# Memory norm inside v's products, mixing and query rounding inside the key/value products, TensorE's order by hand

## The chip, the cores and the metric

The kernel runs on one core of a Trainium2 chip. A core has five engines with instruction streams of their own: TensorE (PE in the profile), VectorE (DVE), ScalarE (ACT), GpSimd (POOL) and SyncE (SP), which issues the DMAs. Each engine works through its stream in order and waits for the others by semaphores. The metric is the device time of one execution in microseconds (us).

## The reference

One layer of a decoder: a half-step feed-forward network, three mixing branches, a half-step feed-forward network. Sequence 1024, width 1024, all in float32. What the change touches is branch A (spatial gating) and branch C (attention into 256 memory tokens):

```python
h = RMSNorm(x); z = h @ W_in            # columns [u | v | c_q | c_kv | k_rope | q_mem | gates]
# A: u * (tril(W_s) v + b), chunks of 128 positions, 8 groups of 64 columns
v = layernorm(gelu(z[v]), ln_g, ln_b).reshape(B, nc, CHUNK, SG_GROUPS, SG_GROUP_DIM)
mixed = jnp.einsum('gts,bcsgd->bctgd', w, v) + b_s.T[None, None, :, :, None]
y_a = u * mixed
# C: cross-attention, 4 heads of 128
q = rmsnorm(q_m.reshape(B, S, MEM_HEADS, MEM_HEAD_DIM), q_norm)
kv = rmsnorm(mem, mem_norm) @ w_kv
k = rmsnorm(kv[..., :MEM_WIDTH].reshape(B, M, MEM_HEADS, MEM_HEAD_DIM), k_norm)
p = softmax(q k^T * MEM_HEAD_DIM ** -0.5);  y_c = p @ kv[..., MEM_WIDTH:]
# merged = sum of sigmoid(gate_i) * (y_i @ W_branch_i);  x = x + merged @ W_out
```

## The kernel before

A float32 product is made of three matmuls (`mm3`, L147 to L149): each operand is split into a rounded high part (fp32r, a cast on ACT, L130) and the rest (a subtraction on DVE, L131), and high·high, low·high and high·low are added up in PSUM. A split of a row thus costs one ACT and one DVE instruction, and a matmul waits for both. `split_gain` (L139, L140) does the same with a factor.

The part around the change runs in this order, and PE goes through it in the middle of the span:

- `sgu` (branch A's gating). `gelu_rows` makes v for half a sequence (512 positions): for each of the 8 slices d of the width, four row blocks, three matmuls each, 96 in all; then Gelu on ACT into the tile `u` (L598). On DVE follow the layer norm's statistics (L634, L635), reciprocal roots in small steps (`rsqrt_steps`, L157 to L168), two passes (L638, L640) and the low half of the split (L131, `v_lo`). This is done for the first half and the second half.
- `mem_norm`, between the two halves in the code: it loads the memory (1 MB, transposed, 256 tokens wide), squares it on ACT (L366, 8 of 128x256) and adds the squares on DVE (L371, 7). After v's products `finish` runs: `token_sums` (a matmul with ones, L380), reciprocal root, `norm_scale` (transposes that spread the factors over the partitions, L392) and `norm_put` (L406 and a split) for 8 slices.
- `mem_kv`: product 1 (keys) and product 2 (values) of the normed memory with 48 matmuls of 512 columns each; `head_norm` on the keys (L670 to L676), `to_feature` (8 transposes, L422; split with a gain).
- Mixing, twice: 8 groups of three matmuls with 256 columns and an ACT copy with bias into a tile `u` (L651); 16 transposes (L657), a product with u (L658) and a split.
- `mem_queries` (L745 squares, L139/L140 rounding, L748 sums of squares on POOL, L751 `pick` matmuls that sum over heads, reciprocal root) and `mem_attention`: scores (S), exponentials on ACT (L778), turning (T, transposes L820) and values (V) for four pairs of row blocks. Between them it takes steps F of a filler, the product of branch A with its weights (`branches`, 16 steps of 12 matmuls).

The pool of `sgu` has one buffer for each name unless said otherwise: the tile `u` exists once, `v_hi` and `v_lo` twice. The order on each engine is set by the framework's scheduler from its own cost figures; `after` adds a dependence that only orders. PE's list of S, T, V and F steps is a request that the scheduler may change. `mm` tiles hold two PSUM banks, `bank` tiles one. All DMAs of this part stand in SP's one queue in the order of issue.

Of the kernel before, what the change touches and what calls it, by code (L numbers as in the profile page):

```python
# [8 lines left out]
F32 = mybir.dt.float32  # L9
# [36 lines left out]
class Kernel:  # L46
# [97 lines left out]
    def mm3(self, out, s, m, first, last, **kw):  # L144

        mmul = self.nc.tensor.matmul
        mmul(out, s[0], m[0], start=first, stop=False, **kw)  # L147
        mmul(out, s[0], m[1], start=False, stop=False, **kw)  # L148
        self.last = mmul(out, s[1], m[0], start=False, stop=last, **kw)  # L149

    def rsqrt_steps(self, v, n):
# [222 lines left out]
    def token_sums(self, acc, late=False, bank=None):  # L374


        n = acc.shape[-1] // P
        b = (bank or self.bank)()[:, :n]
        for t in range(n):
            i = self.nc.tensor.matmul(  # L380
                b[:, t:t + 1], acc[:, t * P:(t + 1) * P], self.ones, start=True, stop=True)
            if late and t == 0:
                self.after(i, self.last)
        return b

    def norm_scale(self, r, late=False, bank=None):


        n = r.shape[-1]
        b = (bank or self.bank)()  # L390
        for t in range(n):
            i = self.nc.tensor.transpose(  # L392
                b[:, t * P:(t + 1) * P], r[:, t:t + 1].to_broadcast([P, P]), self.ident)
            if late and t == 0:
                self.after(i, self.last)
        return b[:, :n * P]

# [196 lines left out]

    def gelu_rows(self, dst, h, w, pairs):


        gelu = lambda d, x: self.nc.scalar.activation(d, x, ACT.Gelu)  # L598
# [8 lines left out]
    def sgu(self, h):  # L607
        nc, a, tc = self.nc, self.a, self.tc
        with tc.tile_pool(name="sgu", bufs=1) as p:
            ln_g = self.bcast_row(p, "ln_g", a["sg_ln_g"], SGW)  # L610
# [10 lines left out]
            vs, norm = [], None  # L621
            for hf in range(2):
                if hf:
                    norm = self.mem_norm()
                vhi, vlo = (p.tile([P, 4, SGW], F32R, name=n, bufs=2) for n in ("v_hi", "v_lo"))
                vs.append((vhi, vlo))
                rows = p.tile([P, 4, SGW], F32, name="u")
                self.gelu_rows(rows, h[hf], w, hf == 0)
                for i in range(0, 4, 2):
# [12 lines left out]
                    self.split(vhi[:, i:i + 2], vlo[:, i:i + 2], v)  # L642
            kv = self.mem_kv(norm())
            yt = [self.split_pair() for _ in range(4)]
            for hf in range(2):
                m, v = p.tile([P, 4, SGW], F32, name="u"), vs[hf]
                for g in range(SGG):
                    b = self.bank()[:, :4 * SGW // SGG].rearrange("p (c d) -> p c d", c=4)
                    cols = slice(g * SGW // SGG, (g + 1) * SGW // SGG)
                    self.mm3(b, (whi[:, g], wlo[:, g]), tuple(x[:, :, cols] for x in v), True, True)  # L650
                    nc.scalar.activation(m[:, :, cols], b, ACT.Identity, bias=self.sg_b[:, g:g + 1])  # L651
                for j in range(4):
                    u = self.row()
                    nc.sync.dma_start(u, self.z[ZU + j][:, hf])
                    b = self.bank()
                    for c in range(4):
                        nc.tensor.transpose(b[:, c * P:(c + 1) * P], m[:, c, j * P:(j + 1) * P], self.ident)  # L657
                    nc.vector.tensor_tensor(u, u, b, op=ALU.mult)  # L658
                    self.split(*(t[:, hf * 512:hf * 512 + 512] for t in yt[j]), u)
        return yt, kv  # L660

# [16 lines left out]
    def mem_norm(self):  # L678


        nc, a = self.nc, self.a
        views = lambda n, dt: [t[:, i].rearrange("p (c m) -> p c m", m=ML)[:, c]
                               for t in (self.h4(dt) for _ in range(n)) for i in range(2) for c in range(2)]
        x4 = [self.h4() for _ in range(2)]
# [7 lines left out]
        hi, lo = views(2, F32R), views(2, F32R)  # L692

        def finish():
            r = self.rms(self.token_sums(acc, late=True), ML // P, D)
            scale = self.norm_scale(r, late=True)
            for c in range(DT):
                self.norm_put(hi[c], lo[c], x[c], self.g_mem[:, c:c + 1], scale)
            return hi, lo

        return finish

    def mem_kv(self, mt):

# [16 lines left out]
        self.head_norm(x, [ps[:, 0], ps[:, 1]])  # L721
        ps = product(w)
        for hh in range(0, MH, 2):
# [6 lines left out]

    def mem_queries(self, p):

# [3 lines left out]
        nc.gpsimd.tensor_scalar(gq, self.mq_g, -MD ** -0.5, None, op0=ALU.mult)  # L736
        qt, b = [], self.bank()[:, :NT * MH]
        for pair in range(MH // 2):
            sq = [p.tile([P, S], F32, name="m4", bufs=3) for n in range(2)]
            for o in range(2):  # L740
                q = self.raw()
                nc.sync.dma_start(q, self.z[ZQ + 2 * pair + o].rearrange("p a w -> p (a w)"))
                qt.append(tuple(p.tile([P, S], F32R, name=n, bufs=MH) for n in ("mq_hi", "mq_lo")))
                for n, t in enumerate(sq):
                    nc.scalar.activation(  # L745
                        t[o * P // 2:(o + 1) * P // 2], q[n * P // 2:(n + 1) * P // 2], ACT.Square)
                self.split_gain(*qt[-1], q, gq)
            nc.gpsimd.tensor_tensor(sq[0], sq[0], sq[1], op=ALU.add)  # L748
            for t in range(NT):
                at = t * MH + 2 * pair  # L750
                nc.tensor.matmul(b[:, at:at + 2], sq[0][:, t * P:(t + 1) * P], self.pick, start=True, stop=True)  # L751
        r = p.tile([P, NT * MH], F32, name="mq_r")
        nc.vector.tensor_copy(r, self.rms(b, NT * MH, MD))
        nr = p.tile([P, NT * MH], F32, name="mq_nr")
        nc.gpsimd.tensor_scalar(nr, r, -1.0, None, op0=ALU.mult)
        return qt, r, nr

    def mem_attention(self, p, queries, kt, vv, filler):

# [4 lines left out]
        def scores(i, k):  # L764
# [42 lines left out]
        yt = [self.split_pair(self.h4) for _ in range(MH)]  # L807
        for f, *x in ((F,), (F,), (F,), (S, 0, 0), (S, 0, 1), (F,), (T, 0, 0), (S, 1, 0), (F,), (T, 0, 1), (S, 1, 1),
                      (F,), (V, 0), (T, 1, 0), (F,), (S, 2, 0), (T, 1, 1), (F,), (S, 2, 1), (F,), (V, 1), (T, 2, 0),
                      (F,), (S, 3, 0), (T, 2, 1), (F,), (S, 3, 1), (F,), (V, 2), (T, 3, 0), (F,), (T, 3, 1), (F,),  # L810
                      (F,), (V, 3)):
            f(*x)
# [149 lines left out]
    def mixer(self, norm):  # L962
# [19 lines left out]

        ya, kv = self.sgu(h)
        with tc.tile_pool(name="mem", bufs=1) as p:
            branch_a = self.branches(0, ya, sink_a)
            queries = self.mem_queries(p)
            yc = self.mem_attention(p, queries, *kv, branch_a)
        each = [(d, f) for d in range(DT) for f in range(2)]
# [974 lines left out]
```

## Time and profile before

| quantity | value |
|---|---|
| time, median of 3 runs | 2222.18 us (2221.76 to 2222.68) |
| time of the profiled execution | 2222.94 us |
| its span (first to last instruction) | 2221.2 us |
| PE busy | 2183.0 us (98%) |
| DVE busy | 1563.5 us (70%) |
| ACT busy | 913.1 us (41%) |
| POOL busy | 249.8 us (11%) |
| mean granted TensorE clock | 0.991 |

A row of a view by line gives the line, engine, operation, tiles, shape and count, then the busy time, the mean of one, and the idle time ahead of it with what ended it. A row of a timeline gives the start, the duration, the instruction and in brackets the wait ahead of it. A row of the windows gives, for a stretch of the span, its length and then for PE, PE's weight loads, DVE, ACT and POOL the busy time (with the count), the granted clock, the share of DMA engines in use and GB/s. Matmuls overlap, so the distance between two starts, not the duration, says what one costs.

### The profile page before, as it was taken

The page shows a single profiled execution, that of the slowest core. Times are in us where ns is not written, and L with a number is a line of the kernel's source. Part 1 is how long each engine was busy: PE and PEld are TensorE (multiplying, and loading weights), DVE is VectorE, ACT ScalarE, POOL GpSimd, SP SyncE. Part 2 cuts the span into 40 slices and gives each one's busy share as a digit, 9 for nine tenths or more (in the row PEclk, how much of TensorE's full clock was granted, in tenths as well). Part 3 has the DMA queues.
Part 4 walks back from the last instruction along what each step waited for, and adds up shares of the span by engine and source line. Part 5 has one row for each costly group of instructions (what it writes and reads, how often), then busy time and mean ns, then how long its engine had stood idle before and what let it go on. Part 6 is the DMA issues. An engine that isn't in the chain of part 4 may idle for free.

```text
span 2221.2 us, 27585 instructions
## 1 busy us (share of the span) xinstructions
PE 2183.0 (98%) x10256; PEld 1819.3 (82%) x10256; DVE 1563.5 (70%) x2406; ACT 913.1 (41%) x1513; POOL 249.8 (11%) x252
## 2 busy tenths in 40 slices
PE   9999999999999999999978999999999999999999
PEld 5788888888887888888857889988888888888887
DVE  7976666579888555545777768885886666657884
ACT  5422222243455333344436448843342222224432
POOL 0012111100000000001300131140002121210000
PEclk9999999999999999999988999999999999999999
DMA  4242333484432333331624650075033333328543
GB/s 144 81 147 96 103 101 106 154 306 149 149 109 95 117 102 114 133 102 44 222 95 152 236 210 30 30 284 202 36 104 110 100 114 100 114 100 299 180 128 104
DMA packets 116086, 294.30 MB, mean 132 GB/s; under 512 B 13680, under 2 KB 22000, under 8 KB 115952
## 3 DMA queue, kind: packets, MB, share of 16 engines
q1 hardware_dynamic: 115952, 292.55, 38.6%
q8 instruction: 80, 1.31, 0.2%
q14 instruction: 54, 0.44, 0.1%
HBM read 206.00 MB, written 86.51 MB: 132 GB/s over the span
## 4 chain that ended last, share of the span: by engine, by line
PE 89%; DVE 7%; ACT 2%; issue 1%; DMA 1%; POOL 0%; SPq 0%; ACTq 0%; DVEq 0%; POOLq 0%
PE one L147 14%; PE one L148 14%; PE one L149 14%; PE bank L147 12%; PE bank L149 12%; PE bank L148 12%; PE mm L149 2%; PE mm L147 2%; PE mm L148 2%; PE bank L902 1%; PE bank L917 1%; PE bank L918 1%; DVE wlo L131 1%; PE bank L422 1%; DVE wlo L136 1%
## 5 line engine op out<-in xcount | busy, mean ns | idle before, releaser
L135 ACT CAST whi<-x 128x1024 fp32r<-128x1024 f32 (+1 forms) x201 | 191.2, 954 | 501.9 <-PE one L148 220.4
L1305 DVE TENSOR_TENSOR t<-t,one 128x512 f32<-128x512 f32 x186 | 127.6, 686 | 244.2 <-PE one L149 243.4
L147 PE MATMUL bank<-h,whi 128*128 128x512 f32 x676 | 263.3, 390 | 0.0
L148 PE MATMUL bank<-h,whi 128*128 128x512 f32 x676 | 263.1, 389 | 0.0
L149 PE MATMUL bank<-h,wlo 128*128 128x512 f32 x676 | 263.0, 389 | 0.0
L136 DVE TENSOR_TENSOR wlo<-x,whi 128x1024 fp32r<-128x1024 f32 (+1 forms) x201 | 239.7, 1194 | 31.7 <-ACT whi L135 31.6
L147 PE MATMUL one<-h,whi 128*128 128x512 f32 x508 | 198.7, 391 | 0.7 <-ACT t L1414 0.7
L149 PE MATMUL one<-h,wlo 128*128 128x512 f32 x508 | 197.7, 389 | 0.0
L148 PE MATMUL one<-h,whi 128*128 128x512 f32 x508 | 197.7, 389 | 0.0
L147 PE MATMUL one<-w,whi 128*128 128x512 f32 x424 | 164.9, 389 | 0.0
L149 PE MATMUL one<-w,wlo 128*128 128x512 f32 x424 | 164.9, 389 | 0.0
L148 PE MATMUL one<-w,whi 128*128 128x512 f32 x424 | 164.9, 389 | 0.0
L130 ACT CAST whi<-w 128x1024 fp32r<-128x1024 f32 (+1 forms) x108 | 95.1, 899 | 144.0 <-PE one L148 62.1
L1707 POOL TENSOR_TENSOR raw<-raw 128x512 f32<-128x512 f32 x38 | 62.9, 1656 | 806.0 <-DVE raw L1553 806.0
L131 DVE TENSOR_TENSOR wlo<-w,whi 128x1024 fp32r<-128x1024 f32 (+1 forms) x108 | 110.1, 1033 | 61.2 <-ACT whi L130 61.1
L149 PEld LDWEIGHTS bank<-h,wlo 128*128 128x128 f32 x676 | 126.9, 188 | 26.4
L148 PEld LDWEIGHTS bank<-h,whi 128*128 128x128 f32 x676 | 126.9, 188 | 26.2
L147 PEld LDWEIGHTS bank<-h,whi 128*128 128x128 f32 x676 | 126.9, 188 | 26.2
L147 PE MATMUL bank<-whi 128*128 128x512 f32 x352 | 136.9, 389 | 0.0
L148 PE MATMUL bank<-wlo,whi 128*128 128x512 f32 x352 | 136.9, 389 | 0.0
L149 PE MATMUL bank<-whi,wlo 128*128 128x512 f32 x352 | 136.9, 389 | 0.0
L147 PEld LDWEIGHTS one<-h,whi 128*128 128x128 f32 x508 | 95.4, 188 | 21.0 <-ACT t L1414 1.1
(372 smaller groups left out, 4898.7 us busy)
## 6 DMA issues: line engine op xcount, KB each, us to landing
x<-in_ffn_w_gu_dram SPq DMA_DIRECT2D x78, 512.0 KB, 5.2
w<-tdt SPq DMA_DIRECT2D x40, 512.0 KB, 4.5
tdb<-raw SPq DMA_DIRECT2D x64, 256.0 KB, 2.1
h<-in_ffn_w_down_dram SPq DMA_DIRECT2D x64, 256.0 KB, 6.0
gate<-raw SPq DMA_DIRECT2D x31, 512.0 KB, 2.6
w<-tdb SPq DMA_DIRECT2D x30, 512.0 KB, 4.7
tdt<-w SPq DMA_DIRECT2D x48, 256.0 KB, 2.1
x<-in_w_gate_dram SPq DMA_DIRECT2D x21, 512.0 KB, 5.7
```

The lines of the kernel that those rows point to most:

```text
L130: self.nc.scalar.copy(hi, src)
L131: return (eng or self.nc.vector).tensor_tensor(lo, src, hi.bitcast(F32), op=ALU.subtract)
L135: self.nc.scalar.copy(hi, src)
L136: return lambda: self.nc.vector.tensor_tensor(lo, src, hi.bitcast(F32), op=ALU.subtract)
L147: mmul(out, s[0], m[0], start=first, stop=False, **kw)
L148: mmul(out, s[0], m[1], start=False, stop=False, **kw)
L149: self.last = mmul(out, s[1], m[0], start=False, stop=last, **kw)
L422: nc.tensor.transpose(b[:m, k * P:(k + 1) * P], s, self.ident)
L902: nc.tensor.transpose(b[:, at:at + P], prs[t][:, kk * P:(kk + 1) * P], self.ident)
L917: nc.tensor.matmul(o, w, pt[0], start=n == 0, stop=False)
L1305: return self.nc.vector.tensor_tensor(out, x, y, op=ALU.add)
L1707: sub = lambda d, x, y: (eng or nc.gpsimd).tensor_tensor(d, x, y, op=ALU.subtract)
```

## The change

Four things are changed. First, `mem_norm` becomes a generator in three steps: the memory is loaded ahead of v's second pair of weights into two larger tiles, squared in 2 ACT instructions of 128x1024 and added up in 3 DVE instructions (128x1024, 128x512, 128x256). The norm's matmuls are put inside v's products by `amid`: the token sums ahead of slice d = 7 of the first half, the spreading of the factors ahead of d = 3 of the second half, and the normed memory is written right after. Second, from the key product to the end of memory attention PE's order is the order of the code (`manual_schedule`); the other engines are still scheduled. Third, mixing is a generator `mix(hf)`, taken between the key product and the value product (matmuls of the first half), inside the value product (its transposes), after it (matmuls of the second half) and after the first step of branch A (its transposes). Fourth, the queries are split into tiles that are used before for other things (`h4`, and `v_hi`/`v_lo` of the halves that are mixed), their squares use the tiles of weights, the softmax rows use four views of `v_hi`/`v_lo`, and the list of S, T, V and F steps is another. The separate pool of memory attention is gone. The tile `u` still exists once.

The core of the diff:

```diff
@@ gelu_rows
-    def gelu_rows(self, dst, h, w, pairs):
+    def gelu_rows(self, dst, h, w, pairs, amid={}):
         for d in range(DT):
+            then = amid[d]() if d in amid else None
             for i in range(4):
                 b = ps[i // 2][:, i % 2] if pairs else ps[i]
-                self.mm3(b, tuple(x[:, i * P:(i + 1) * P] for x in h[d]), w[d], d == 0, d == DT - 1)
+                first = self.mm3(b, tuple(x[:, i * P:(i + 1) * P] for x in h[d]), w[d], d == 0, d == DT - 1)
+                if then:
+                    self.after(first, then)
+                then = None
@@ sgu
+            mem = self.mem_norm()
+            next(mem)
             w = self.load(a["w_v"])
...
+            take(0, {7: lambda: next(mem)})
+            take(1, {3: lambda: next(mem)})
+            m0, m1 = mix(0), mix(1)
+            with tc.manual_schedule(engines={mybir.EngineType.PE}):
+                kv = self.mem_kv(next(mem), (lambda: next(m0, None), lambda: next(m0, None)))
+                rooms = [v8(n).rearrange("p (a b) w -> p a (b w)", a=2) for n in ("v_hi", "v_lo")]
+                queries = self.mem_queries([(x[:, 0], x[:, 1]) for x in rooms])
+                next(queries)
+                next(m1)
...
+                branch = self.branches(0, yt, sink)
+                next(branch)
+                next(m1, None)
+                yc = self.mem_attention(next(queries), rooms, *kv, branch)
@@ mem_norm
+        for n, t in enumerate(x4):
+            sq = self.x4() if n == 0 else sq2
+            nc.scalar.activation(sq, t, ACT.Square)
...
+        nc.vector.tensor_tensor(first, first, sq2, op=ALU.add)
+        nc.vector.tensor_tensor(acc, first[:, 0].rearrange("p (a m) -> p a m", a=2),
+                                first[:, 1].rearrange("p (a m) -> p a m", a=2), op=ALU.add)
+        nc.vector.tensor_tensor(acc[:, 0], acc[:, 0], acc[:, 1], op=ALU.add)
+        yield
...
-        acc = None
-        for c in range(DT):
-            acc = self.norm_feed(acc, x[c], ML)
@@ mem_kv
-        def product(w):
+        def product(w, then=None):
...
+                if d == DT // 2 - 1 and then:
+                    then()
...
         self.head_norm(x, [ps[:, 0], ps[:, 1]])
-        ps = product(w)
+        amid[0]()
+        ps = product(w, amid[1])
@@ mem_attention
-            pr = p.tile([P, MH * ML], F32, name="m4", bufs=3).rearrange("p (h m) -> p h m", h=MH)
+            pr = rooms[t % len(rooms)]
...
-        for f, *x in ((F,), (F,), (F,), (S, 0, 0), (S, 0, 1), (F,), (T, 0, 0), (S, 1, 0), (F,), (T, 0, 1), (S, 1, 1),
...
+                (F,), (F,), (S, 0, 0), (F,), (S, 0, 1), (F,), (T, 0, 0), (S, 1, 0), (F,), (T, 0, 1), (S, 1, 1), (F,),
```

The order on PE around the memory norm, before: behind the last of v's matmuls (into `bank_8647`) stand the token sums and the spread factors, then the key product (`mm_8880`).

```order
L149 MATMUL bank_8647<-whi_8449,h4_5175 128x512
L380 MATMUL bank_8800<-ones_91,t_8614 128x1 [waits Activation_49]
L380 MATMUL bank_8800<-ones_91,t_8614 128x1
L392 MATMUL bank_8817<-ident_86,rs_y_8805 128x128 [waits DVE_49,Activation_49]
L392 MATMUL bank_8817<-ident_86,rs_y_8805 128x128
L147 MATMUL mm_8880<-whi_8850,h4_8637 128x512 [waits PE_49,Activation_49]
```

The same two pairs after the change: the factors (`rs_y_8561`) are spread inside the second half of v's matmuls, ahead of slice 3; the sums (L381) stand likewise inside the first half.

```order
L148 MATMUL bank_8645<-wlo_8446,h4_5158 128x512
L149 MATMUL bank_8645<-whi_8445,h4_5159 128x512
L394 MATMUL mm_8682<-ident_86,rs_y_8561 128x128 [waits DVE_49,Activation_49]
L394 MATMUL mm_8682<-ident_86,rs_y_8561 128x128
L147 MATMUL bank_8642<-whi_8445,h4_5158 128x512
L148 MATMUL bank_8642<-wlo_8446,h4_5158 128x512
```

So no matmul of the norm stands between v's products and the key product any more. The order on PE at the end of the mixing matmuls after the change: behind the key product follow the 8 groups of the first half (`bank_8982` to `bank_9017`), of which the fifth is `bank_9002`; before, the value product stood here, and the mixing followed `to_feature`.

```order
L147 MATMUL bank_8997<-v_hi_8467,x4_8419 128x256 [waits Activation_49]
L148 MATMUL bank_8997<-v_lo_8468,x4_8419 128x256
L149 MATMUL bank_8997<-v_hi_8467,x4_8420 128x256
L147 MATMUL bank_9002<-v_hi_8467,x4_8419 128x256 [waits Activation_49]
L148 MATMUL bank_9002<-v_lo_8468,x4_8419 128x256
L149 MATMUL bank_9002<-v_hi_8467,x4_8420 128x256
```

The mixing's matmuls alternate over four banks, so the fifth group waits for the ACT copy of the first. That copy (now L661) writes the tile `u`, in ACT's order after the change:

```order
L130 CAST v_hi_8639<-u_8641 128x1024 [waits DVE_49]
L784 ACTIVATE wlo_9151<-raw_9152 64x1024 [waits DMAHW1_49,Pool_49]
L130 CAST v_hi_8639<-u_8641 128x1024 [waits DVE_49]
L661 ACTIVATE u_8981<-bank_8982,c_sg_b_3207 128x4x64 [waits DVE_49,PE_49]
L661 ACTIVATE u_8981<-bank_8987,c_sg_b_3207 128x4x64 [waits PE_49]
```

`u_8981` takes the one buffer of `u_8641`, the rows of the second half of v. The first copy's wait on DVE is for the last reading of `u_8641`, the second `v_lo_8640`. In DVE's order after the change the rows ahead of it are these (`rs_y_8785`, `rs_y_8811` the layer norm's factors, `rs_y_8960` and `h4_8948` the key's head norm):

```order
L649 SCALAR_TENSOR_TENSOR u_8641<-u_8641,rs_y_8811,ln_b_8414 128x512 [waits DVE_49]
L649 SCALAR_TENSOR_TENSOR u_8641<-u_8641,rs_y_8811,ln_b_8414 128x512
L167 SCALAR_TENSOR_TENSOR rs_b_8962<-rs_w_8961 128x8 [waits DVE_49]
L131 TENSOR_TENSOR v_lo_8640<-u_8641,v_hi_8639 128x1024 [waits Activation_49]
L169 SCALAR_TENSOR_TENSOR rs_y_8960<-rs_b_8962,rs_y_8960 128x8 [waits DVE_49]
L703 TENSOR_TENSOR h4_8948<-h4_8948,rs_y_8960 128x1024 [waits DVE_49]
L131 TENSOR_TENSOR v_lo_8640<-u_8641,v_hi_8639 128x1024 [waits Activation_49]
```

Between the first statistics of v's first half and that `v_lo` DVE now has the splits of seven of the eight slice pairs of the key and value weights (14 instructions of 128x512), the low halves of the normed memory and the keys' head norm; before, it had four of the pairs (8 instructions) and neither of the others.

More of the change, by code (lines that the diff above doesn't have):

```diff
@@ L146, in mm3 @@
         mmul = self.nc.tensor.matmul
-        mmul(out, s[0], m[0], start=first, stop=False, **kw)
+        i = mmul(out, s[0], m[0], start=first, stop=False, **kw)
         mmul(out, s[0], m[1], start=False, stop=False, **kw)
         self.last = mmul(out, s[1], m[0], start=False, stop=last, **kw)
+        return i
     def rsqrt_steps(self, v, n):
@@ L383, in token_sums @@
                 self.after(i, self.last)
+        self.final = i
         return b
@@ L619, in sgu, with take @@
             self.split(whi, wlo, ws)
+            mem = self.mem_norm()
+            next(mem)
             w = self.load(a["w_v"])
[L621 to L625, printed above, removed]
+            vs, yt = [], []
+            def take(hf, amid={}):
+                vhi, vlo = (v8(n) for n in ("v_hi", "v_lo"))
                 vs.append((vhi, vlo))
                 rows = p.tile([P, 4, SGW], F32, name="u")
-                self.gelu_rows(rows, h[hf], w, hf == 0)
+                self.gelu_rows(rows, h[hf], w, hf == 0, amid)
                 for i in range(0, 4, 2):
@@ L642, in sgu, with mix @@
                     self.split(vhi[:, i:i + 2], vlo[:, i:i + 2], v)
-            kv = self.mem_kv(norm())
-            yt = [self.split_pair() for _ in range(4)]
-            for hf in range(2):
+            def mix(hf):
+                if not yt:
+                    yt.extend(self.split_pair() for _ in range(4))
                 m, v = p.tile([P, 4, SGW], F32, name="u"), vs[hf]
@@ L659, in sgu @@
                     self.split(*(t[:, hf * 512:hf * 512 + 512] for t in yt[j]), u)
-        return yt, kv
+            take(0, {7: lambda: next(mem)})
[7 more added lines that the diff above has]
+                next(m1)
+                rooms = [v8(n, F32) for n in ("v_hi", "v_lo")]
+                rooms = [x.rearrange("p (a h) (b m) -> p a (h b) m", a=2, b=2)[:, k] for x in rooms for k in range(2)]
+                branch = self.branches(0, yt, sink)
+                next(branch)
+                next(m1, None)
+                yc = self.mem_attention(next(queries), rooms, *kv, branch)
+        return yc
     def head_norm(self, x, ps):
@@ L736, in mem_queries @@
         nc.gpsimd.tensor_scalar(gq, self.mq_g, -MD ** -0.5, None, op0=ALU.mult)
-        qt, b = [], self.bank()[:, :NT * MH]
+        qt, ss = [], []
         for pair in range(MH // 2):
-            sq = [p.tile([P, S], F32, name="m4", bufs=3) for n in range(2)]
+            sq = [self.wide(n).bitcast(F32) for n in ("whi", "wlo")]
             for o in range(2):
@@ L742, in mem_queries @@
                 nc.sync.dma_start(q, self.z[ZQ + 2 * pair + o].rearrange("p a w -> p (a w)"))
-                qt.append(tuple(p.tile([P, S], F32R, name=n, bufs=MH) for n in ("mq_hi", "mq_lo")))
+                qt.append(rooms.pop(0) if pair else self.split_pair(self.h4))
                 for n, t in enumerate(sq):
@@ L748, in mem_queries, with mem_attention @@
             nc.gpsimd.tensor_tensor(sq[0], sq[0], sq[1], op=ALU.add)
+            ss.append(sq[0])
+        yield
+        b = self.bank()[:, :NT * MH]
+        for pair, sq in enumerate(ss):
             for t in range(NT):
                 at = t * MH + 2 * pair
-                nc.tensor.matmul(b[:, at:at + 2], sq[0][:, t * P:(t + 1) * P], self.pick, start=True, stop=True)
-        r = p.tile([P, NT * MH], F32, name="mq_r")
+                nc.tensor.matmul(b[:, at:at + 2], sq[:, t * P:(t + 1) * P], self.pick, start=True, stop=True)
+        r = self.const.tile([P, NT * MH], F32, name="mq_r")
         nc.vector.tensor_copy(r, self.rms(b, NT * MH, MD))
-        nr = p.tile([P, NT * MH], F32, name="mq_nr")
+        nr = self.const.tile([P, NT * MH], F32, name="mq_nr")
         nc.gpsimd.tensor_scalar(nr, r, -1.0, None, op0=ALU.mult)
-        return qt, r, nr
-    def mem_attention(self, p, queries, kt, vv, filler):
+        yield qt, r, nr
+    def mem_attention(self, queries, rooms, kt, vv, filler):
         nc = self.nc
@@ L981, in sink_c @@
                 nc.sync.dma_start(mc[d], rows)
[L983 to L987, printed above, removed]
+        with tc.tile_pool(name="sgu", bufs=1) as p:
+            yc = self.sgu(h, p, sink_a)
         each = [(d, f) for d in range(DT) for f in range(2)]
```

39 lines of the change are left out of this document (24 added, 15 removed).

## The prediction

> **What bounds the kernel now.** I read the page's busy shares first (TensorE is busy for 98% of the span), so a change can only win where TensorE waits or runs at a lowered clock. The windows of the stretch from v's products to memory attention show where that is:
>
> ```profile
> 1119.50:1134.00 14.50, 1.61 (x8) 1.15 (x7) 14.50 (x55) 5.70 (x10) 0.00 (x0) 0.59 0.23 73
> 1134.00:1142.50 8.50, 6.22 (x14) 4.49 (x15) 6.59 (x15) 2.31 (x7) 0.00 (x0) 0.50 0.00 0
> ...
> 1161.30:1173.60 12.30, 11.53 (x89) 10.39 (x87) 8.94 (x14) 10.88 (x24) 0.00 (x0) 1.00 0.20 60
> 1173.60:1190.40 16.80, 10.47 (x42) 9.26 (x42) 11.28 (x11) 15.03 (x18) 4.51 (x2) 0.59 0.59 189
> 1190.40:1215.00 24.60, 23.82 (x133) 20.21 (x133) 18.71 (x37) 11.81 (x32) 0.53 (x2) 1.00 0.46 142
> 1215.00:1256.00 41.00, 41.00 (x258) 36.74 (x259) 30.48 (x53) 23.71 (x68) 2.15 (x2) 1.00 0.42 135
> 1256.00:1308.00 52.00, 52.00 (x242) 43.50 (x241) 26.30 (x50) 10.40 (x28) 21.58 (x20) 1.00 0.91 349
> ```
>
> Length less TensorE's busy time is its idle time: 12.9, 2.3, 0.8, 6.3 and 0.8, together 23.1 us. Busy time times (1 − granted clock) is what the clock cost: 1.61 × 0.41 + 6.22 × 0.50 + 10.47 × 0.41 = 8.1 us. So 31.2 us are lost here, the ceiling of any gain. After 1215 TensorE never idles, but from 1256 the DMA engines are 0.91 busy, which leaves little room there for a later start. The chain of waits on TensorE names the losses:
>
> ```profile
> PE bank L392 <- DVE rs_y L168: 8.5, 1, 8.5
> PE mm L147 <- ACT mq_hi L139: 5.2, 2, 4.0
> PE bank L380 <- ACT u L598: 2.4, 1, 2.4
> PE mm L149 <- DVE h L131: 2.3, 1, 2.3
> ```
>
> The first, third and fourth belong to the memory norm behind v's products, the second to the rounding of the queries. But what ends the first is VectorE, and VectorE was not idle:
>
> ```profile
> 1105.40:1138.00 32.60, 17.74 (x73) 13.61 (x71) 32.53 (x103) 14.38 (x26) 0.00 (x0) 0.76 0.25 81
> ...
> 1105.47 1.29 DVE L634 BATCH_NORM_STATS2 bn<-u 128x6 f32<-128x512 f32 x2 [2.96 <-ACT u L598]
> ...
> 1137.83 2.76 DVE L131 TENSOR_TENSOR h<-h,h 128x256 fp32r<-128x256 f32 x8
> ```
>
> It is busy 32.53 of 32.60 us, from the statistics of v's first half to the end of `v_lo` of the second, at 1137.8. That chain, 32.4 us long, is what I follow. TensorE waits only because it needs something that lies on it.
>
> **The memory norm moved into v's products.** It takes away the waits of L380, L392 and L149: 13.2 us. ScalarE's squares and VectorE's adds (8 and 7 before; 2 and 3 now) get cheaper, and off TensorE's path either way. It also moves the memory's two loads ahead of the second pair of v's weights in SyncE's queue. The transfers that this can hold back:
>
> ```profile
> h<-in_mem_dram SPq DMA_DIRECT2D x2, 512.0 KB, 7.7
> raw<-gate SPq DMA_DIRECT2D x4, 512.0 KB, 3.5
> raw<-in_w_branch_dram SPq DMA_DIRECT2D x6, 256.0 KB, 2.9
> ```
>
> Against a 512 KB load at 3.5 us the memory's take 7.7 (transposing). The order now puts the three adds and the norm's small steps ahead of a weight split that v's first half needs and of its statistics. The adds cost about 2.3 us (1.2 for 1024 columns, 0.7 for 512, 0.4 for 256, from the rows below). So VectorE's chain starts later by between 0 and 5 us (all hidden; adds and a late load); I take 2.5, at 1108.0, the adds alone.
>
> **Mixing moved between the products.** A group's copy on ScalarE writes the single tile `u`, so the first copy waits for the last `v_lo` of v's second half, and the fifth group of matmuls waits for the first copy. That is the new wait. That `u` holds its next writer back is seen already: this Gelu, with four banks done, waited for `v_lo`.
>
> ```profile
> 1121.29 2.06 ACT L598 ACTIVATE u<-bank 128x512 f32<-128x512 f32 x4 [0.60 <-DVE v_lo L131]
> ```
>
> When does that `v_lo` end now? The chain gains, by the order on VectorE, 6 splits of weights (14 against 8), the 8 low halves of the normed memory, two sums of the head norm, its scaling, and some ten steps on columns:
>
> ```profile
> L131 DVE TENSOR_TENSOR wlo<-raw,whi 128x512 fp32r<-128x512 f32 x8 | 5.2, 679 | 0.0
> ...
> L131 DVE TENSOR_TENSOR h<-h,h 128x256 fp32r<-128x256 f32 x8 | 2.8, 410 | 0.0
> ...
> L672 DVE TENSOR_REDUCE hn_ss<-t 128x4 f32<-128x512 f32 x2 | 1.4, 686 | 1.7 <-ACT t L670 1.7
> L676 DVE TENSOR_TENSOR h<-h,rs_y 128x1024 f32<-128x1024 f32 x1 | 1.2, 1224 | 0.1
> L164 DVE SCALAR_TENSOR_TENSOR rs_w<-rs_b,rms_v 128x8 f32<-128x8 f32 x2 | 0.3, 166 | 0.1
> ```
>
> 6 × 0.65 = 3.9, then 2.8, 1.4, 1.2, and 10 × 0.08 (half of 166 ns, since they overlap) = 0.8, together 10.1. The ten steps of the memory norm's own root, 0.8, leave the chain, since they now run ahead of it; its eight scalings (L406) are in it both times. That is 9.3 more: the chain is 41.7 us long and ends at 1149.7. There is no gap in it that could take any of this, by the 32.53 of 32.60.
>
> POOL's sum of the queries' squares (2.37 us) now falls into this chain, and VectorE does not run beside it:
>
> ```profile
> 1188.25 2.37 POOL L748 TENSOR_TENSOR m<-m,m 128x1024 f32<-128x1024 f32 x1 [6.22 <-ACT m L745]
> ...
> 1188.85 2.32 DVE L131 TENSOR_TENSOR wlo<-raw,whi 128x512 fp32r<-128x512 f32 x1 [1.51 <-ACT whi L130]
> ```
>
> A split of 0.68 us took 2.32 beside it: 1.64 more. The collision costs between 0 and 2.4 us; I take 1.0, since some of VectorE's instructions there read PSUM or columns. The Trainium skill (SBUF — State Buffer, "SBUF: two separate sides") says that a VectorE instruction with two SBUF inputs and one of GpSimd lock each other out for the whole instruction; these two rows agree, and by that rule the cost would be the full 2.4, so that the time would be 1.4 us longer than the sum below.
>
> ```profile
> 1118.89 0.39 PE L148 MATMUL bank<-wlo,h 128*128 128x512 f32 x1
> 1119.12 0.39 PE L149 MATMUL bank<-whi,h 128*128 128x512 f32 x1
> ...
> 1138.30 0.80 PE L149 MATMUL mm<-whi,h 128*128 128x512 f32 x1 [2.28 <-DVE h L131]
> ...
> 1142.67 0.39 PE L147 MATMUL mm<-whi,h 128*128 128x512 f32 x1
> ...
> 1177.50 0.58 PE L147 MATMUL mm<-h,mq_hi 128*128 128x256 f32 x1 [3.95 <-ACT mq_hi L139]
> ...
> 1203.87 0.28 PE L149 MATMUL mm<-h,mq_lo 128*128 128x256 f32 x1
> 1203.99 0.28 PE L147 MATMUL mm<-h,mq_hi 128*128 128x256 f32 x1
> ...
> 1205.07 1.03 PE L820 MATMUL bank<-ident,m 128*128 128x128 f32 x8
> ```
>
> A matmul of 512 columns takes 0.23 us from start to start (1118.89 to 1119.12), one of 256 columns 0.12. With the first copy (0.5, and as much until its end is seen) TensorE resumes at 1151.7. Without any wait it would reach the fifth group at 1119.35, the end of v's products, + 1.0 (an allowance) for the norm's few small matmuls + 48 × 0.227 for the key product + 12 × 0.12 for four groups = 1132.7. So 19.0 us are lost up to there, wherever the waits lie.
>
> After such an idle time the clock is half: from 1138.30 TensorE ran without a gap and was at the full clock, with 0.39 instead of 0.63 for a matmul, 4.4 us later. Nearly half of that, 2.0 us, is lost at the new restart (between 1.6 and 5.5, the latter if gaps follow, as from 1177.50 to 1190.4, where 10.47 × 0.41 plus the gaps' share was lost). The Trainium skill (TensorE: Matmul & The Clock Gate, "What's actually happening") gives about 3.4 us of idle time for the fall and as much dense work for the return; the wait of 3.95 ahead of 1177.50 and the 4.4 us agree roughly, and by its figure 1.7 us would be lost here.
>
> **Query rounding moved.** The waits on `mq_hi` (5.2), `mq_lo` and the second slow spell go: the queries are rounded while TensorE is in the value product. What is late next is the second mixing. Its first copy stands on ScalarE behind the keys' two gains, a split of a branch weight and the values' cast:
>
> ```profile
> L139 ACT ACTIVATE h<-bank,c_mem_k_norm 128x512 fp32r<-128x512 f32 x2 | 1.3, 684 | 7.0 <-PE bank L422 7.0
> ...
> L130 ACT CAST whi<-raw 128x512 fp32r<-128x512 f32 x28 | 16.4, 625 | 23.1 <-PE mm L149 10.7 <-PE bank L149 6.2 <-DMA raw<-in_mem_w_kv_dram 3.0
> ...
> L130 ACT CAST h<-mm 128x1024 fp32r<-128x1024 f32 x1 | 1.0, 1016 | 0.0
> ...
> L139 ACT ACTIVATE mq_hi<-raw,m_gq 128x1024 fp32r<-128x1024 f32 x4 | 4.6, 1143 | 0.0
> ```
>
> 1.3 + 0.6 + 1.0 + 0.5 = 3.4 us behind the keys' transposes, of which four groups (1.4) cover a part: 2.0 us waited. Two roundings of queries of 1.1 each stand between later copies: 2.0 more. So 4.0 (2 to 6) are lost, in pieces too short for the clock. At the first turn I add 0.7 (VectorE's share of a softmax row is late by one instruction). The new list of steps adds nothing on TensorE, but TensorE can no longer take other work when a softmax row is late, and the DMA engines are nearly full right behind: between 0 and 2 us are given back; I take 0, since the nearest rows, from 1215 to 1308, show TensorE idle for nothing. The tile moves themselves cost nothing: same instructions, same shapes.
>
> **The sum.** Lost before 31.2; after 19.0 + 2.0 + 4.0 + 0.7 = 25.7. The gain is 5.5 us. The profiled execution took 2222.94 us, 0.8 above the median of the runs, 2222.18, and 1.7 above its span: against the median, 2216.7 us. A measurement of this kernel tells about 0.2% (4.4 us) from no change, so this is only just on the faster side.
>
> **The rivals.** (B) A second slow spell, slower than before. The second mixing's first copy also stands behind the split of a branch weight, whose load waits in SyncE's queue behind the last queries' load and several mixing rows. If that load lands late enough that the 2.0 us piece becomes 4 or more, past the 3.95 that were followed by half clock, the clock falls again: the wait itself 2 to 5 (a load of 7.7 instead of 2.9), the clock 5.5 at the rate of the stretch before 1190.4. Together 7.5 to 10.5 more: 2224.2 to 2227.2. For it speaks that this load comes after two 512 KB loads in series; against it that the stretch had the DMA engines only 0.2 to 0.6 busy.
>
> (C) Faster: the wait on `u` comes out shorter. If the chain starts where it did (−2.5), POOL's sum hits nothing (−1.0), and the copies of the second mixing run ahead of the transposes (−2 to −4), the gain is 11 to 13: 2209 to 2211. The chain's arithmetic speaks against more, since VectorE has no gap to shorten.
>
> (D) The list of memory attention gives something back, by softmax rows that come late:
>
> ```profile
> L773 DVE TENSOR_REDUCE m_mx<-mm 128x4 f32<-128x1024 f32 x4 | 4.8, 1207 | 0.0
> L783 DVE TENSOR_TENSOR m<-m,m_rs 128x1024 f32<-128x1024 f32 x3 | 3.7, 1222 | 0.2
> ```
>
> A turn follows its scores by a reduction (1.2), four exponentials and a scaling (1.2), some 4 to 5 us in all; a filler step of 12 matmuls (12 × 0.227 = 2.7) covers most of it. Three such waits of 2 us make 2222.7, no change; with five it is 2226.7, slower. Against it: the first two turns have one step F more ahead of them than before. That the change does not do what it says is not open: the orders show the matmuls in their new places.
>
> **How the numbers follow.** The forecast has 0.55 (0.36 faster by over 0.2%, 0.19 within, since its own range, 2212 to 2221, straddles the bound), B 0.20 (0.13 slower, 0.07 within), C 0.13 (all faster), D 0.12 (0.05 within, 0.07 slower). That makes 0.49 faster, 0.31 within 0.2%, 0.20 slower. The range 2209 to 2227 takes in most of B, C and D; what it leaves out is C's best and B's worst, and mishaps together.
>
> **What would show it.** Right: no wait of L394 longer than 1 us; one wait of about 15 us on the fifth mixing group, ended by ScalarE's copy (L661), which itself waits for `v_lo`; VectorE busy nearly throughout from 1108 to 1150; half clock for some 4 us after; the first turn at about 1201 (1205.1, less 31.2 − 25.7 = 5.5, plus 1.3 for twelve matmuls that are 0.11 dearer than those they replace ahead of it). Wrong: that wait under 10 us or over 20, a granted clock below 0.7 again after 1165, turns that wait in memory attention, or TensorE idle behind 1215.

## The result: no change that can be measured

The changed kernel takes 2222.57 us (median of 12 runs, 2221.14 to 2223.38), the kernel before 2222.34 us in the same runs: the ratio is 1.000, with a 95% interval from 0.9991 to 1.0009. A gain of 5.5 us to 2216.7 was forecast. The span of the profiled execution is 2221.0 us (2221.2 before), the mean granted clock 0.992 (0.991).

The waits of TensorE from 1070 to 1320 in the changed kernel: who waits, for whom, us in all, times, the longest.

```profile
PE bank L147 <- ACT u L661: 14.3, 2, 13.4
PE mm L147 <- ACT v_lo L821: 3.2, 1, 3.2
PE mm L148 <- DVE wlo L131: 2.5, 1, 2.5
PE bank L147 <- DVE h L140: 2.2, 1, 2.2
PE mm L147 <- ACT v_hi L821: 1.2, 1, 1.2
PE mm L147 <- DVE a_mx L923: 1.0, 1, 1.0
PE bank L863 <- DVE m_mx L817: 0.8, 1, 0.8
PE mm L147 <- ACT v L524: 0.2, 1, 0.2
```

All waits of the memory norm behind v's products (8.5, 2.4, 2.3, 2.0) and those on the query rounding are gone. In their place stands one of 13.4 us, on the copies into `u`, and some of 1 to 3 us, two of them in memory attention, where before there was only one, of 0.2 us. (The wait on `a_mx` was there before too, 1.0 us.) Four rows of TensorE's timeline give the places, and a row of the windows for VectorE:

```profile
1149.97 0.58 PE L147 MATMUL bank<-v_hi,x 128*128 128x256 f32 x1 [13.36 <-ACT u L661]
...
1169.43 0.39 PE L147 MATMUL bank<-v_hi,x 128*128 128x256 f32 x1 [2.16 <-DVE h L140]
...
1200.35 1.06 PE L863 MATMUL bank<-ident,v_hi 128*128 128x128 f32 x8 [0.82 <-DVE m_mx L817]
...
1237.27 0.39 PE L147 MATMUL mm<-h,h 128*128 128x256 f32 x1 [3.20 <-ACT v_lo L821]
```

```profile
1106.00:1149.40 43.40, 30.61 (x142) 25.39 (x140) 43.14 (x119) 24.62 (x40) 2.56 (x1) 0.88 0.41 133
```

The first turn is at 1200.35; it was at 1205.07. So 4.7 us were in hand there, and 6.0 if the 1.3 us of dearer work ahead of it is counted. The first scores of the causal attention follow later, ahead of them TensorE waits for `a_mx` in both kernels; here the two are level again, 1312.58 before and 1312.38 now:

```profile
1312.58 0.44 PE L147 MATMUL mm<-h,h 96*128 96x384 f32 x1 [0.97 <-DVE a_mx L880]
```

```profile
1312.38 0.44 PE L147 MATMUL mm<-h,h 96*128 96x384 f32 x1 [0.97 <-DVE a_mx L923]
```

So between the two places 4.5 us of the lead and the 1.3 us of work done ahead were given back, 5.8 us in all, in memory attention. The windows of the changed kernel show it: in the first of these rows TensorE is idle for 4.4 us, and the clock falls for a time; before, it was busy for all of 1215 to 1256.

```profile
1205.00:1256.00 51.00, 46.56 (x297) 41.61 (x296) 37.98 (x67) 27.73 (x80) 2.29 (x2) 0.97 0.34 114
1256.00:1308.00 52.00, 52.00 (x233) 43.07 (x232) 23.62 (x44) 9.76 (x26) 20.21 (x19) 1.00 0.89 335
```

### The profile page after: what moved, and what is told of

The parts are those of the page before. It is cut to its first block, busy times and chain, and to the rows that moved or that the text cites. A ratio compares the mean times of both kernels' runs of the same rounds, so it can differ in the third digit from the quotient of the medians.

```text
span 2221.0 us, 27576 instructions
## 1 busy us (share of the span) xinstructions
PE 2180.9 (98%) x10256; PEld 1818.3 (82%) x10256; DVE 1564.4 (70%) x2402; ACT 912.7 (41%) x1507; POOL 249.0 (11%) x252
```

## The experiments

Each is an edit of the changed kernel, and all compute the whole reference. The kernel before took 2222.3 to 2222.6 us beside them.

**Rows of their own.** The rows of v's second half stand in two tiles of another pool instead of `u`.

```diff
-                rows = p.tile([P, 4, SGW], F32, name="u")
+                rows = [self.x4() for _ in range(2)] if hf else p.tile([P, 4, SGW], F32, name="u")
...
-                    v = rows[:, i:i + 2]
+                    v = rows[i // 2] if hf else rows[:, i:i + 2]
```

> The changed kernel, with the rows of v's second half in two tiles of the x4 kind instead of the tile u, so that mixing's copies need not wait for them. Theory 1 (the single tile u makes the 13.4 us wait, and what lies behind it is free by 1152): the wait on the fifth mixing group falls under 2 us; the value product runs in its place; TensorE then waits 1 to 3 us for the keys' head norm or v_lo, since VectorE's chain ends at about 1150 as before; the first turn comes 8 to 12 us earlier (1188 to 1192 instead of 1200.3), and the time falls by 4 to 12 us to about 2214. Theory 2 (the wait moves on: the queries' loads and roundings on ScalarE and VectorE hold the second mixing and the scores): the first turn comes less than 3 us earlier, the time is within 2 us of 2222.5.

Measured: ratio 0.9963 (0.9951 to 0.9976), median 2212.89 us. The wait on the fifth group is 1.1 us and the first turn at 1194.10. Theory 1 holds for the wait, though the first turn came only 6.3 us earlier, less than the 8 to 12 expected. Two things can account for it, and their shares are open. The traced execution was the slowest of the five, 2217.46 us, and it came to this part 1.3 us later (the first Gelu into `u` starts at 1106.22 instead of 1104.94). And ScalarE's queue has squares of the queries (L784, 1.06 each) between mixing's copies, so that TensorE still has short waits on `u`. Its waits up to 1165:

```profile
PE bank L147 <- ACT u L661: 3.9, 3, 1.8
PE mm L148 <- DVE wlo L131: 2.5, 1, 2.5
PE bank L147 <- DVE h L140: 0.5, 1, 0.5
```

**Another list in memory attention.** From the first value step on a filler step stands again between a turn and the scores behind it.

```diff
-                (V, 0), (T, 1, 0), (S, 2, 0), (F,), (T, 1, 1), (S, 2, 1), (F,), (V, 1), (T, 2, 0), (S, 3, 0), (F,),
-                (T, 2, 1), (S, 3, 1), (F,), (V, 2), (T, 3, 0), (F,), (T, 3, 1), (F,), (V, 3)):
+                (V, 0), (T, 1, 0), (F,), (S, 2, 0), (T, 1, 1), (F,), (S, 2, 1), (F,), (V, 1), (T, 2, 0), (F,),
+                (S, 3, 0), (T, 2, 1), (F,), (S, 3, 1), (F,), (V, 2), (T, 3, 0), (F,), (T, 3, 1), (F,), (F,), (V, 3)):
```

> The changed kernel with another list of steps from the first value step on: one filler step again between each T and the S behind it. Theory D (the list gives back what was gained: S waits for the exponentials that free its PSUM tile): the waits of 3.2 and 1.2 us on the exponentials go, the half clock around 1237 too, and the time falls by 4 to 6 us, to 2217 to 2218.5. Rival (the stretch from 1256 on, with its DMA engines 0.89 busy, sets the end): TensorE then waits 3 us or more behind 1245, and the time stays within 1.5 us of 2222.5.

Measured: ratio 0.9976 (0.9967 to 0.9985), median 2216.72 us. Both waits on the exponentials are gone, and TensorE is busy throughout at the full clock:

```profile
1205.00:1256.00 51.00, 51.00 (x318) 45.50 (x316) 41.31 (x72) 30.22 (x84) 2.56 (x2) 1.00 0.42 142
```

The first turn (1200.60) and the 13.2 us on `u` are as they were. So the list alone gave back 5.9 us, and the nearly full DMA engines behind 1256 took none of it. How it comes about is seen on ScalarE in the changed kernel, rows of its timeline:

```profile
1233.67 0.59 ACT L130 CAST whi<-bank 128x512 fp32r<-128x512 f32 x1 [3.00 <-PE bank L863]
1234.15 0.38 ACT L130 CAST h<-mm 128x256 fp32r<-128x256 f32 x1
1234.41 0.60 ACT L130 CAST whi<-bank 128x512 fp32r<-128x512 f32 x1
1234.89 0.59 ACT L821 ACTIVATE v_lo<-mm,m_mx,mq_nr 128x256 f32<-128x256 f32 x1
```

ScalarE stands for 3.00 us at the cast of a turn that TensorE has not made yet. Behind the cast stand the four exponentials, and only they free the PSUM tile that the next scores (1237.27) need: there are two such `mm` tiles. With a filler step between, the exponentials are over in time. The shorter wait, 1.2 us at 1220.83, has the same form: ahead of its exponentials ScalarE stood 2.14 us at a cast (`h<-mm`, 1218.20) that waited for VectorE.

**Mixing behind the value product.**

```diff
-                kv = self.mem_kv(next(mem), (lambda: next(m0, None), lambda: next(m0, None)))
+                kv = self.mem_kv(next(mem), (lambda: None, lambda: None))
+                next(m0)
+                next(m0, None)
```

> The changed kernel with the mixing of the first half put behind the value product and the keys' transposes, as before the change; all else as changed. Theory 1 (the chain on VectorE to the last v_lo ends near 1149 whatever TensorE does, and the value product of 11 us fits ahead of it): the wait on the fifth group falls to under 2 us, a wait of 2 to 4 us on the head norm appears ahead of the keys' transposes, the first turn comes 6 to 10 us earlier and the time falls by 4 to 10 us. Theory 2 (mixing earlier is worth its place): the time rises or stays within 2 us of 2222.5, since the query rounding becomes the last.

Measured: ratio 0.9954 (0.9942 to 0.9967), median 2212.58 us, the first turn at 1189.31. Undoing this part of the change gains 10 us, and the first turn comes 11.0 us earlier, a little more than the 6 to 10 expected. The value product fills the time in which TensorE waited for `u`; in the first mixing the wait on `u` is 0.4 us, and ahead of the keys' transposes TensorE waits 0.4 us on the head norm, less than the 2 to 4 expected.

**The memory norm behind v's products.** The norm's two groups of matmuls are taken after v's products; mixing stays.

```diff
-            take(0, {7: lambda: next(mem)})
-            take(1, {3: lambda: next(mem)})
+            take(0)
+            take(1)
+            next(mem)
+            next(mem)
```

> The changed kernel with the memory norm's two groups of matmuls behind v's products, as before the change; mixing stays between the products. Theory 1 (TensorE waits for one chain on VectorE, so a wait ahead of the key product only takes its time from the wait on u): waits of about 8 to 13 us come back ahead of the key product, the wait on the fifth mixing group shrinks by about as much, and the time stays within 3 us of 2222.5. Rival (the norm's move is worth its 13 us by itself): the wait on the fifth group stays over 10 us and the time rises by 8 to 13 us.

Measured: ratio 1.0033 (1.0020 to 1.0045), median 2229.70 us, 7.1 above the changed kernel. This lies between both theories. Its waits up to 1165:

```profile
PE mm L394 <- DVE rs_y L169: 8.4, 1, 8.4
PE bank L147 <- ACT u L661: 5.3, 1, 5.3
PE mm L149 <- DVE h L131: 3.1, 1, 3.1
PE bank L381 <- ACT u L601: 2.7, 1, 2.7
PE mm L147 <- ACT h L130: 2.0, 1, 2.0
```

16.2 us of waits are back, but the wait on `u` falls only by 8.1 us, from 13.4 to 5.3, and the 2.5 us in v's first half go. `v_lo` was done at 1137.6, yet the first copy came at 1156.62, right behind the head norm's four ScalarE instructions (from 1152.39 on, after the late key product) and two squares of queries. So the wait on `u` is not set by VectorE's chain alone; once that is short, ScalarE's order sets it.

**Both out.** The last two edits together.

> The changed kernel with the memory norm's matmuls behind v's products and the first mixing behind the value product, both as before the change; the queries' tiles, TensorE's fixed order and the list as changed. The fourth corner of a square: changed 2222.6, mixing out 2212.6, norm out 2229.7. Theory 1 as amended (the norm's waits of 13 to 16 us cost in full where no wait on u stands behind them to be shortened): 10 to 14 us above mixing out, 2222 to 2227. Rival (the norm's move is worth the same 7 us wherever the mixing stands): 2219 to 2221.

Measured: ratio 1.0018 (1.0009 to 1.0027), median 2225.43 us, 12.9 above mixing out. With that the square is closed: moving the norm into v's products is worth 12.9 us where mixing stands behind the value product and 7.1 where it stands ahead of it; moving the mixing ahead costs 10.0 us with the norm inside and 4.3 with the norm outside. The forecast named both the norm's waits that go and the new wait on `u`, but did not ask what either part would be worth without the other. The account closes: with both parts out the rest of the change costs about 3 us against the kernel before, the norm inside takes 12.9 off, the mixing ahead puts 10.0 on, and that leaves nothing. The list's share of the rest is 5.9 us, by the second experiment, so all else (the queries' rounding, the fixed order) saves about 3 us; this last figure is a difference and was not run by itself.

**The scheduler's order on TensorE.** `manual_schedule` is taken away.

```diff
-            with tc.manual_schedule(engines={mybir.EngineType.PE}):
+            if True:
```

> The changed kernel without the fixed order on TensorE: the scheduler orders it. If the scheduler moves the value product ahead of the mixing groups that wait for u, the wait of 13.4 us shrinks under 5 and the time falls by 5 to 10 us: then the order by hand costs time. If it keeps the mixing there (its own cost figures show no wait), the wait stays near 13 us and the time is within 3 us of 2222.5.

Measured: ratio 0.9951 (0.9939 to 0.9964), median 2211.64 us. The scheduler puts the whole value product between the fourth and the fifth group:

```order
L147 MATMUL bank_8995<-v_hi_8467,x4_8419 128x256 [waits Activation_49]
L148 MATMUL bank_8995<-v_lo_8468,x4_8419 128x256
L149 MATMUL bank_8995<-v_hi_8467,x4_8420 128x256
L147 MATMUL mm_9020<-whi_8916,h4_8685 128x512 [waits PE_49]
L148 MATMUL mm_9020<-wlo_8917,h4_8685 128x512
```

That is the place of the wait on `u`, and it shrinks to 1.7 us at most. The waits on the exponentials (L821) are gone too, so the gain holds both losses. The fixed order, as it is written, costs 11 us, a little more than the 5 to 10 expected.

**Both losses mended, in two ways.** Rows of their own with the list of filler steps, and mixing behind the value product with that list.

> The changed kernel with both edits: the rows of v's second half in tiles of their own (that edit alone: 2212.9) and the list with a filler step between each T and the S behind it (alone: 2216.7). If the two losses are separate, in order on TensorE and neither hidden by the other, the gains of 9.5 and 5.6 add up: 2205.5 to 2209. If the second loss is there only to absorb what the first frees (a bound behind both, such as the transfers from 1256 on), the time stays at 2211 or above.

> The changed kernel with the first half's mixing behind the value product (alone: 2212.6) and the list with filler steps (alone: 2216.7). By the same reasoning 2205 to 2209; it ends within 2 us of the kernel with rows of their own and the same list, since both remove the same wait.

Measured: 0.9932 (0.9920 to 0.9944), 2207.24 us, and 0.9933 (0.9919 to 0.9946), 2207.25 us. The gains add up: 0.9963 × 0.9976 = 0.9939 and 0.9954 × 0.9976 = 0.9930. The two losses are separate, and nothing behind them takes either gain back. Both kernels beat the kernel before and the changed one by 15 us.

**Weights first.** In the last of these, v's weights are issued ahead of the memory's loads.

```diff
-            mem = self.mem_norm()
-            next(mem)
             w = self.load(a["w_v"])
+            mem = self.mem_norm()
+            next(mem)
```

> The kernel of mixing out and the list with filler steps (2207.2), with v's weights issued ahead of the memory's loads: one of the two memory loads then stands behind the third slice pair of v's weights in SyncE's queue. It asks what the wait of 2.6 us in v's first half is, which the change brought. If it comes from the memory's load and its add ahead of the weights' split on VectorE, it falls under 1.5 us and the time to 2204.5 to 2206.5. If it comes from VectorE's q and k work, which stands ahead of both, it stays over 2 us and the time within 1.5 us of 2207.2.

Measured: 0.9924 (0.9910 to 0.9938), 2206.34 us. The time does not tell it from 2207.25; the waits up to 1150 do. First without, then with the edit:

```profile
PE mm L148 <- DVE wlo L131: 2.6, 1, 2.6
PE bank L425 <- DVE h L705: 1.2, 1, 1.2
```

```profile
PE bank L425 <- DVE h L705: 3.2, 1, 3.2
PE mm L148 <- DVE wlo L131: 0.9, 1, 0.9
```

The wait in v's first half loses 1.7 us, and the wait on the head norm, 60 us later, gains 2.0. The memory's load and its add, which stood ahead of that split, were the cause of the first. The time was not won because VectorE's chain did not start any earlier. It starts behind the first Gelu into `u`, and this came 28.5 us after v's first matmul without the edit (1075.07 to 1103.60) and 28.6 with it (1077.60 to 1106.16): it waits for a store, as shown below. What TensorE does not wait for early, it then waits for late.

**Rows of their own and the scheduler's order.**

> The changed kernel with rows of their own for v's second half and no fixed order on TensorE. With the fixed order and the list of the change it took 2212.9, with the fixed order and filler steps 2207.2; with the free order and the single u 2211.6. If the free order is good because it avoids the wait on u and spaces the scores, both of which these edits do by hand, then 2206 to 2211, no better than 2207.2 by more than 1.5. If the order by hand costs something else too, under 2205.

Measured: 0.9935 (0.9921 to 0.9949), 2208.84 us: as good as the mended orders by hand and no better. So no cost of the order by hand beyond the two losses shows.

## Why the prediction was right and wrong

- **What bounds the kernel, and the new wait: right.** The wait of 13.4 us is at the fifth mixing group, for the first copy into `u`, which waits for `v_lo`. "About 15" was forecast. VectorE's chain ran from 1106.00 to 1149.3, busy 43.14 of 43.40 us; the forecast had 1108.0 to 1149.7, and 1150.7 with POOL's sum. The chain was 43.3 us instead of 41.7 plus 1.0. Its start was 2.0 us earlier than assumed, and the reason given for the start was wrong: the adds held a split in v's first half (the wait of 2.5 us), not the statistics. These follow the first Gelu into `u`, and it waits for the last store of `q`, an older tile. Before the change and after it:

```profile
1104.41 1.94 ACT L598 ACTIVATE u<-mm 128x1024 f32<-128x1024 f32 x2 [3.03 <-DMA qd<-q]
1104.94 1.95 ACT L601 ACTIVATE u<-mm 128x1024 f32<-128x1024 f32 x2 [17.07 <-DMA qd<-q]
```

It is the same in all ten experiments. Presumably `u` takes room that `q` had; no run gave `u` other room there. The memory's loads did not hold it up either. The prediction calls them transposing, at 7.7 us, but the host lays the memory out transposed, and in the changed kernel they land in 4.3 us.
- **POOL's sum: right in kind, low in size.** It fell into the chain and made four passes of the layer norm 4.81 us instead of 2.74 long. That is 2.07 us, not the 1.0 taken, and near 2.4, the upper end that was given.

```profile
1140.85 4.81 DVE L649 SCALAR_TENSOR_TENSOR u<-u,rs_y,ln_b 128x512 f32<-128x512 f32 x4
1141.23 2.56 POOL L787 TENSOR_TENSOR whi<-whi,wlo 128x1024 f32<-128x1024 f32 x1 [40.32 <-ACT wlo L784]
```

- **The restart: right in kind, a little high.** Behind 1149.97 the twelve matmuls of the last four groups took 2.72 us instead of 12 × 0.12 = 1.44, and the first of 512 columns 0.38 instead of 0.23: 1.4 us lost; 2.0 was taken.
- **The second mixing: near in idle time, wrong in place and on the clock.** It waited 2.2 and 0.9 us, 3.1 instead of 4.0. But the forecast had the wait on mixing's copies, and only the 0.9 is there. The 2.2 us are on VectorE: the third group needs the PSUM bank of the keys' transposes, and VectorE had a query's gain and three splits of mixed rows ahead of the keys' gain (L140) that frees it. And "in pieces too short for the clock" failed: from 1170.08 to 1176.7 the clock was half, and again from 1183.96, behind the sums over heads. By the count of slow matmuls that cost some 2.5 and 1.5 us. Of rival B the late load came true, as ScalarE stood 2.63 us for a branch weight in front of the first copy, but not what it was to cause: TensorE waited only 0.9 us for that copy, and the clock had fallen ahead of that wait.
- **Up to the first turn: right.** 1201 was forecast, 1200.35 came. The errors above (wait and restart too long by about 2 us, the clock's 4.0 us behind them left out, and others) cancel, which is luck in part.
- **Memory attention: the step that failed.** "The new list of steps adds nothing on TensorE" and, of "between 0 and 2 us", "I take 0". The list gave back 5.9 us, as the edit of the list alone shows, so rival D, which had 0.12, is what happened on top of the forecast. Its place and its size were right (2222.7 with three waits of 2 us), its mechanism was not: D has turns that wait for late softmax rows, and one turn waited, 0.8 us. What waited 1.2 and 3.2 us were scores. The prediction looked at how many filler steps stand between scores and their turn, where by its count the first two turns have one more than before; it did not look at the other distance, from the turn to the next scores, which need a PSUM tile that the exponentials free. That distance had lost its filler step in four places, and TensorE waited in two of them, with the clock lowered for a time behind the longer wait. With the list mended the kernel took 2216.72 us, and 2216.7 was forecast without that loss; an agreement this close is luck, given the errors above.
- **Chances:** no change had 0.31, the likeliest case was a gain.

Open stays why TensorE's clock fell at 1170, after a wait of only 2.2 us. The length of a wait does not settle it. The wait in v's first half was 2.53 to 2.57 us in the changed kernel and in seven experiments; the clock was half behind it in four of these eight traces (0.63 us for a matmul of 512 columns) and full in the others (0.39). First the experiment with another list, then the one with mixing behind the value product:

```profile
1083.77 0.50 PE L148 MATMUL mm<-wlo,h 128*128 128x512 f32 x1 [2.55 <-DVE wlo L131]
1084.10 0.39 PE L149 MATMUL mm<-whi,h 128*128 128x512 f32 x1
```

```profile
1084.35 0.80 PE L148 MATMUL mm<-wlo,h 128*128 128x512 f32 x1 [2.56 <-DVE wlo L131]
1084.95 0.63 PE L149 MATMUL mm<-whi,h 128*128 128x512 f32 x1
```

So these traces show falls behind waits shorter than the 3.95 us that the forecast went by, and what a wait of some 2.5 us costs cannot be told beforehand from them. Open is also what the chain's start would be worth: no run let the first Gelu go ahead of the store of `q`.

## What to carry to other kernels

An engine that is saturated for 40 us sets when the others get on, so ask first what starts its chain (here a store). Work that needs the chain's end gains nothing from an earlier place, and a tile with a single buffer is where the wait comes up, as with the mixing; work that can be finished ahead of the chain's start does gain, as the memory norm's sums. In an order by hand look at each step for both things it needs, its input and the buffer it writes, and put independent work (the value product, a filler step) ahead of the one that is later. A change that measures as nothing can hold gains and losses of some 10 us each: undo its parts one by one, and in pairs.

## What the runs showed of the hardware

The sums over heads are 32 TensorE instructions of 2 columns, 3.75 us, without a wait among them. Behind them the clock was half, though no idle time was recorded there. Rows of the timeline of the changed kernel:

```profile
1178.61 1.91 PE L668 MATMUL bank<-ident,u 128*128 128x128 f32 x16
1180.35 3.75 PE L794 MATMUL bank<-pick,whi 128*128 128x2 f32 x32
1183.96 0.77 PE L147 MATMUL bank<-x,whi 128*128 128x512 f32 x1
1184.53 0.63 PE L148 MATMUL bank<-x,whi 128*128 128x512 f32 x1
```

The same stands in all ten experiments (with the norm moved out two matmuls later), here with the mixing moved back:

```profile
1169.30 3.80 PE L796 MATMUL bank<-pick,whi 128*128 128x2 f32 x32
1172.96 0.77 PE L147 MATMUL bank<-x,whi 128*128 128x512 f32 x1
```

A matmul of 512 columns took 0.63 us there instead of 0.39. It lasted some 3.4 us (1183.96 to 1187.36) and cost about 1.5 us. The kernel before makes these sums in two groups of 16, and behind the second, 1.84 us long and in the midst of matmuls of 512 columns, the clock stayed full:

```profile
1194.09 1.84 PE L751 MATMUL bank<-pick,m 128*128 128x2 f32 x16
1195.79 0.49 PE L147 MATMUL bank<-x,whi 128*128 128x512 f32 x1
```

The 16 transposes alone (1158.31, 1.9 us) were followed by the full clock too, by matmuls of 0.39 to 0.40 us. So in these traces a TensorE without recorded idle time is not always busy enough for the clock: 32 instructions on 2 columns in a row, behind 16 transposes, were not. Whether their columns or the length of the stretch decides was not taken apart.
